# The S5 branch in plain fp32: two pairs of groups in halves of the array, both steps' outputs from the preceding state, D inside an input product

## The chip, the cores and the metric

The kernel runs on one core of one Trainium2 chip. The metric is the device time of one execution in microseconds; the median of 3 runs before the change is 3122.24 us (3120.36 to 3122.88). Beside the runs there is one profiled execution, whose trace spans 3125.4 us from its first to its last instruction. PE is the matmul engine (PEld its weight loads), DVE the vector engine, ACT the scalar engine, POOL the GpSimd, SP the engine that issues most DMAs.

## What is computed

One layer over 1024 tokens of 2048 channels: RMSNorm, an input projection into two branches and gates, an S5 state-space branch, a gated DeltaNet branch, up-projections, a gated merge, an output projection, a residual, and a last RMSNorm. The change is in the S5 branch. It has 64 groups of 16 channels with 64 complex states each, and is linear up to the GELU:

```python
bu_re = jnp.einsum("blgc,gpc->blgp", ug, bb_re)
bu_im = jnp.einsum("blgc,gpc->blgp", ug, bb_im)
...
_, _, s_re, s_im = lax.associative_scan(combine, (a_re, a_im, bu_re, bu_im), axis=1)
y = (jnp.einsum("blgp,gcp->blgc", s_re, _f32(c_re))
     - jnp.einsum("blgp,gcp->blgc", s_im, _f32(c_im)))
y = y.reshape(bsz, l, D_S5) + _f32(d_skip) * u
y = jax.nn.gelu(y)
y = y * jax.nn.sigmoid(y @ _f32(w_glu))
return y * jax.nn.silu(z)
```

## The kernel before

The tokens are taken in two passes of 512. In each pass the big projections are 128x512 products in float32r, a reduced form of fp32 that takes one run through the array: every weight chunk and every activation is split into a hi and a lo part, and each product is three (hi by hi, hi by lo, lo by hi). These "large products" stand on PE in the order of a list of units (q, k, v, z of one head, merge gates, u of one S5 tile, and so on). Weights stream in halves of 512 KB through three buffers `raw`; ACT writes `whi`, DVE writes `wlo`, one chunk for every 12 large products.

Everything else is background work, written as generators: the S5 tiles, the delta rule's preparation and chain, epilogues. After each three large products `pump` lets every lane take one step, if a planner's clock (class `Clock`, a rough model of the engines) says that what the step needs is ready and that DVE isn't too far ahead. So the planner decides where between the large products a step is written; in the program each engine's order is then fixed, and semaphores keep the data right.

S5 works on 8 tiles of 128 channels per pass, each tile 4 pairs of groups. Time is taken in double steps, so a pass has 256 of them:

- `s5_setup` (L593) makes the constants once, in the first pass: the input matrix of each pair (both steps of a double step, hi in `vh_d`, lo in `vl_d`), the output matrices `ft_d` and a product `q0_d` of an output and an input matrix, all kept in DRAM. Its 64 products for `q0_d` are 32 columns wide.
- `s5_epi` (L853) splits u of a tile into hi and lo, even and odd steps, and stores it stacked by pairs (`us_d`) and as it is (`uf_d`).
- `s5_load` (L872) brings `us_d`, `vh_d`, `vl_d` from POOL's queue, `q0_d` and `ft_d` from SP's.
- `s5_gen` (L885), for each pair: an input product of four float32r products (two on 128 rows, two on 64) into bank 6; on DVE a rotation by tables of cos and sin, two scans, the rotation back, into `sx`; then five fp32 products into 32 columns of bank 7. The even step's output comes from the preceding state and the input (`q0`), the odd step's from the state at that step. After four pairs come D times u (two DVE operations on `uf_d`), the GELU, a split into hi and lo, and a store to `yg_d`.

Banks 6 and 7 belong to S5. The delta rule has small fp32 products of its own; the prediction uses two of its loops in `d_prep`. At L1172 four products in one 32x32 strip of the array follow each other, then four in the next. At L1204 two strips take turns, product by product:

```python
for c in range(4):
    PE.matmul(pu[o:o + 32, c, 0:32], lhsT=gs[o + 32:o + 64, c, 0:32], ...)
    PE.matmul(pu[o + 32:o + 64, c, 0:32], lhsT=U[o + 32:o + 64, c, o + 32:o + 64], ...)
```

All instructions are recorded through one helper, so the profile gives L134 for each; groups are told apart by the names of their tiles. `G0a` and `G0b` are the two blocks that hold all S5 tiles, `p` is PSUM, `M` the delta rule's block, `X` and `Y` the activations, `Y` also the scratch of the setup.

Of the kernel before, what the change touches and what calls it, by code (L numbers as in the profile page):

```python
# [36 lines left out]
P = 128  # L37
T = 512          # tokens per pass
NPASS = 2
KT = 16          # k tiles of D_MODEL  # L40
# [53 lines left out]
class Timed:  # L94
# [3 lines left out]
    def __getattr__(self, name):  # L98
# [4 lines left out]
        def g(*a, **k):  # L103
# [6 lines left out]
            if self.key == "PE":  # L110
                if name == "transpose":
                    c = 0.11
                elif k["rhs"].dtype == F32R:
                    c = n / 2400
                else:
                    c = max(n / 600, 0.06) * (0.3 if o.shape[0] <= 32 else 0.5 if o.shape[0] <= 64 else 1.0)
# [30 lines left out]
def kernel(  # L147
# [83 lines left out]
    causal = cpool.tile([P, P], F32, name="causal")      # 1 where partition <= column  # L231
# [20 lines left out]
    vec = cpool.tile([P, 121], F32, name="vec")   # per-channel vectors, one column per tile  # L252
# [16 lines left out]
    vh_d = dram.tile([32, 64, 256], F32, name="vh_d")  # L269
    vl_d = dram.tile([32, 64, 256], F32, name="vl_d")  # L270
    us_d = dram.tile([8, 4, P, 256], F32, name="us_d")   # tile, pair, (hi/lo, even/odd, channel), step
    uf_d = dram.tile([8, P, 1024], F32, name="uf_d")
    ft_d = dram.tile([8, P, 512], F32, name="ft_d")
    q0_d = dram.tile([32, 32, 32], F32, name="q0_d")
    cs_d = dram.tile([32, P, 512], F32, name="cs_d")
    # [4 chunks, 129 rows, 128]: with a row of padding the diagonal blocks lie at one stride
# [4 lines left out]
    ts_d = dram.tile([16, P, T], F32, name="ts_d")  # L281

# [8 lines left out]
    def exp_parts(xin, n, scr):  # L291
        """s, q with exp(x) = s + s*q, on a [128, n] tile; scr: [128, 5n] of scratch."""
# [17 lines left out]
        # two factors, so that the result underflows as exp does  # L310
# [24 lines left out]
    # Half units of [128, 1024]; each gives two chunks of [128, 512], split into hi and lo.  # L335
# [41 lines left out]
    # the first two units share their k loop, and so their chunks alternate  # L377
# [21 lines left out]
    def w_prep():  # L399
# [42 lines left out]
    now = [0.0]            # head being projected, with the share of its units done  # L442
# [34 lines left out]
    def later(o, i):  # L477
        """a store, issued once its data should be there"""
# [114 lines left out]
    def s5_setup(ga, gb, yb):  # L593
        """ga, gb, yb: scratch of [128, 5120], [128, 3072] and [128, 8192]."""
# [66 lines left out]
        # input factor (abar - 1) / lam  # L661
# [14 lines left out]
        # turns per double step, 2 * theta / (2 pi), as fhi + flo  # L676
# [14 lines left out]
        def cmul(dst, c_re, c_im, a_re, a_im):  # L691
            """dst(ri, half) <- c * a; dst returns output views by half of the partitions"""
# [21 lines left out]
        for q4_ in range(8):  # L714
            oo = ((t1f, t2f), (bre_f, bim_f))
            for i in range(2):
# [6 lines left out]
                o, o2 = oo[i][0][0:64, :], oo[i][1][0:64, :]  # L723
                S.activation(o.bitcast(F32R), pb[0:64, :], AF.Copy)
                tt(o2.bitcast(F32R), pb[0:64, :], o, SUB)
            yield
            for i in range(2):
                q2 = 2 * q4_ + i
                for d, o in zip((vh_d, vl_d), oo[i]):
                    SP.dma_start(d[2 * q2:2 * q2 + 2].rearrange("q k m -> k q m"),  # L730
                                 o[0:64, :].rearrange("k (q m) -> k q m", q=2))
# [3 lines left out]
        ft = yb[:, 3072:7168].rearrange("p (i f m) -> p i f m", i=8, f=4)  # L735
# [11 lines left out]
        for i in range(8):  # L747
# [6 lines left out]
        v1 = yb[:, 0:1024].rearrange("p (i q m) -> p i q m", i=8, q=4)  # L754
# [34 lines left out]
    s5w = {}  # L789
# [874 lines left out]
```

## Time and profile before

| what | value |
|---|---|
| median of 3 runs | 3122.24 us |
| span of the profiled execution | 3125.4 us |
| mean granted PE clock | 0.996 |
| input products of S5 (`p<-G0b`, 256 columns) | 256 records, 4 for each pair |
| output products of S5 (`p<-G0a` and `p<-G0b,G0a`, 32 wide, 256 columns) | 640 records, 10 for each pair |
| DMA | 140 GB/s on average |

A product in float32r leaves one record on PE, one in plain fp32 two. The records of PE overlap, since a product is recorded until its last result has gone through the array; what a product costs is read from the distance between starts, not from the length of its record. In the timeline a row merges neighbouring instructions of one kind: its start, the time to the end of the last one, and their number.

### The profile page before, as it was taken

How to read it: one execution, taken by the hardware profiler on the slowest of the kernel's cores; microseconds unless marked ns; L12 is line 12 of the kernel's file. 1: busy time of each engine (PE TensorE's matmuls, PEld its weight loads, DVE VectorE, ACT ScalarE, POOL GpSimd, SP SyncE). 2: the span in 40 equal slices, each digit the busy share in tenths (PEclk: the TensorE clock that was granted, in tenths of full speed). 3: DMA queues.
4: the chain of work that ended last, by engine and by line, in shares of the span. 5: the costliest groups of instructions: out<-in, count | busy, mean ns of one | idle time of the engine just before them, and what ended most of it. 6: DMA issues, size and time to landing. Idle time of an engine off the chain costs nothing.

```text
span 3125.4 us, 43212 instructions
## 1 busy us (share of the span) xinstructions
PE 3091.6 (99%) x16222; PEld 2435.1 (78%) x16222; DVE 1689.8 (54%) x3124; ACT 1140.8 (37%) x2445; POOL 482.7 (15%) x922
## 2 busy tenths in 40 slices
PE   8999999999999999999999999999999999999998
PEld 6887777777777788888877777777777788888887
DVE  5756667766766522553453575566556543226542
ACT  5454444444443222334333334333333322223331
POOL 3432122312200000000042221222122000000000
PEclk9999999999999999999999999999999999999999
DMA  6554545555455644446355455535545564445541
GB/s 163 150 156 119 132 114 127 148 135 144 111 153 162 195 118 124 146 142 219 122 168 136 110 135 133 148 104 136 147 112 141 137 199 132 118 122 152 176 170 56
DMA packets 608980, 438.24 MB, mean 140 GB/s; under 512 B 60489, under 2 KB 535810, under 8 KB 606850
## 3 DMA queue, kind: packets, MB, share of 16 engines
q1 hardware_dynamic: 584962, 406.11, 45.8%
q0 software_dynamic: 23808, 29.37, 4.4%
q8 instruction: 128, 2.10, 0.3%
q14 instruction: 82, 0.67, 0.1%
HBM read 355.05 MB, written 80.35 MB: 139 GB/s over the span
## 4 chain that ended last, share of the span: by engine, by line
PE 91%; DMA 3%; DVE 1%; ACT 1%; POOL 1%; issue 1%; SPq 0%; DVEq 0%; POOLq 0%; ACTq 0%
PE p L134 91%; DMA G0b<-vl_d 2%; POOL M L134 1%; DVE M L134 1%; ACT M L134 0%; SPq L134 0%; POOL G0b L134 0%; DMA vh_d<-G0b 0%; DVE tmp L134 0%; ACT whi L134 0%; DMA raw<-in_w_in_dram 0%; DVE wlo L134 0%; DVE G0a L134 0%; DMA out_dram<-M 0%; ACT G0b L134 0%
## 5 line engine op out<-in xcount | busy, mean ns | idle before, releaser
L134 PE MATMUL p<-X,whi 128*128 128x512 f32 (+1 forms) x4432 | 1401.6, 399 | 1.9 <-DVE whi L134 0.8
L134 DVE TENSOR_TENSOR wlo<-raw,whi 128x512 fp32r<-128x512 f32 x920 | 633.0, 701 | 688.9 <-ACT whi L134 686.8
L134 PEld LDWEIGHTS p<-X,whi 128*128 128x128 f32 (+1 forms) x4432 | 801.5, 188 | 179.7 <-issue 19.2
L134 PE MATMUL p<-X,wlo 128*128 128x512 f32 (+1 forms) x2184 | 853.3, 391 | 0.3 <-DVE wlo L134 0.2
L134 ACT ACTIVATE whi<-raw 128x512 fp32r<-128x512 f32 x917 | 558.0, 625 | 593.2 <-PE p L134 561.3
L134 PE MATMUL p<-Y,whi 128*128 128x512 f32 (+1 forms) x1808 | 571.7, 398 | 0.9 <-ACT p L134 0.9
L134 PEld LDWEIGHTS p<-X,wlo 128*128 128x128 f32 x2184 | 411.4, 188 | 89.6 <-DVE wlo L134 0.9
L134 PEld LDWEIGHTS p<-Y,whi 128*128 128x128 f32 (+1 forms) x1808 | 328.0, 187 | 74.7 <-issue 7.4
L134 PE MATMUL p<-Y,wlo 128*128 128x512 f32 x896 | 350.2, 391 | 0.0
L134 ACT ACTIVATE tmp<-p 128x512 f32<-128x512 f32 x160 | 95.6, 597 | 480.4 <-PE p L134 469.9
L134 POOL TENSOR_SCALAR smalls<-smalls 128x4 f32<-128x4 f32 (+1 forms) x58 | 16.8, 289 | 1377.3 <-DVE smalls L134 1104.2
L134 POOL TENSOR_TENSOR M<-M 32x28 f32<-32x28 f32 (+8 forms) x492 | 182.2, 370 | 268.6 <-DMA M<-lu_d 215.8
L134 DVE TENSOR_TENSOR G0a<-G0a 128x256 f32<-128x256 f32 (+1 forms) x432 | 211.0, 525 | 3.8
L134 PEld LDWEIGHTS p<-M 32*32 32x32 f32 (+2 forms) x3072 | 153.1, 123 | 66.8 <-ACT M L134 27.9
L134 PEld LDWEIGHTS p<-Y,wlo 128*128 128x128 f32 x896 | 168.3, 188 | 36.8 <-DVE wlo L134 0.3
L134 PE MATMUL p<-M 32*32 32x32 f32 (+3 forms) x3072 | 186.9, 215 | 2.5 <-DMA M<-tu_d 1.0
L134 ACT ACTIVATE M<-p 32x128 f32<-32x128 f32 (+3 forms) x337 | 99.2, 298 | 181.7 <-PE p L134 175.6
L134 DVE TENSOR_TENSOR G0a<-p,G0a 128x512 f32<-128x512 f32 x128 | 82.3, 685 | 129.1 <-PE p L134 129.0
L134 PE MATMUL p<-G0a 128*32 128x256 f32 x512 | 133.1, 382 | 0.0
L134 DVE SCALAR_TENSOR_TENSOR tmp<-tmp,vec 128x512 f32<-128x512 f32 x144 | 112.1, 778 | 20.5 <-ACT tmp L134 17.1
L134 PEld LDWEIGHTS p<-G0a 128*32 128x32 f32 x512 | 50.9, 109 | 62.4 <-issue 7.6
L134 DVE TENSOR_TENSOR_SCAN G0a<-rho,scar,G0a 128x256 f32<-128x256 f32 x128 | 90.2, 746 | 0.0
(212 smaller groups left out, 2879.1 us busy)
## 6 DMA issues: line engine op xcount, KB each, us to landing
raw<-in_w_in_dram SPq DMA_DIRECT2D x324, 512.0 KB, 4.0
raw<-in_w_out_dram SPq DMA_DIRECT2D x56, 512.0 KB, 3.9
raw<-in_dn_w_up_dram SPq DMA_DIRECT2D x32, 512.0 KB, 4.2
raw<-in_s_w_up_dram SPq DMA_DIRECT2D x32, 512.0 KB, 3.9
td_d<-tmp SPq DMA_DIRECT2D x32, 256.0 KB, 2.0
M<-tu_d SPq DMA_DIRECT2D x32, 256.0 KB, 3.9
cs_d<-G0a SPq DMA_DIRECT2D x32, 256.0 KB, 3.1
G0b<-us_d POOLq DMA_DIRECT2D x16, 512.0 KB, 7.5
```

The source lines that it names most:

```text
L134: return f(*a, **k)
```

## The change

- The input product of a pair is plain fp32 on the 64 rows of its inputs (2 steps x 2 groups x 16 channels); `vh_d`, `vl_d` and the hi and lo of u are gone. Two pairs are taken together: one in rows 0 to 63, the other in rows 64 to 127, into banks 6 and 7.
- Both steps' outputs come from the state before the double step, so the output matrices are C times A and C times A squared, 64 columns for a pair (2 steps x 32 channels). The two pairs' products go to columns 0 to 63 and 64 to 127.
- What the two steps' inputs add to both outputs, D included, is one product on the whole array with a 128x128 matrix for two pairs (`w0_d`), which the setup makes with 128 products 32 or 64 columns wide.
- u is stored once, in fp32, with even and odd steps apart (`uf_d` is gone). The tile's loads are on SP's queue, with two buffers for u, `ft` and `w0`; the next tile's are issued behind the second two pairs' input product if its u is there by then.
- y stays with even and odd steps apart up to the last merge; the epilogues of z, of the S5 gate and of the last sum read or write every second element instead.
- The planner's clock prices an fp32 product on up to 64 rows at half.

The core of the diff:

```diff
@@ s5_setup
-            S.activation(ft[:, i, 2, :], pb[:, 0:P], AF.Copy)
-            S.activation(ft[:, i, 3, :], pb[:, P:2 * P], AF.Copy, scale=-1.0)
...
+        G.memset(gb[:, 0:2048], 0.0)
+        yield
+        for hf in range(2):
+            pb = bank((6, 7)[hf])
+            pw = pb.rearrange("p (j e c) -> p j e c", j=8, e=2)
+            for j in range(8):
+                for a in range(2):
+                    pr = 2 * (hf * 8 + j) + a
+                    for e in range(2):
+                        for ri in range(2):
+                            m = nb[:, pr, ri].rearrange("p e g c -> p (e g c)")
+                            PE.matmul(pw[64 * a:64 * a + 32 + 32 * e, j, e, :], lhsT=m[:, 0 if e else 32:64],
+                                      rhs=ft[:, pr, ri, 1, :], start=(ri == 0), stop=(ri == 1))
+                if j % 2 == 1:
+                    yield
...
+        for j in range(16):
+            wj = w0[:, j].rearrange("p a e c -> p (a e c)")
+            stt(wj, ident, dd[:, j:j + 1], wj, MUL, ADD)
@@ s5_load
-        G.dma_start(us, us_d[t].rearrange("q p n -> p q n"))
-        for hh in range(2):
-            G.dma_start(vh[64 * hh:64 * hh + 64], vh_d[4 * t:4 * t + 4].rearrange("q k m -> k q m"))
-            SP.dma_start(q0[64 * hh:64 * hh + 32], q0_d[4 * t:4 * t + 4].rearrange("q k m -> k q m"))
-        G.dma_start(vl, vl_d[4 * t:4 * t + 4].rearrange("(a b) k m -> (b k) a m", b=2))
-        SP.dma_start(ft, ft_d[t].rearrange("p (f m) -> p f m", f=4))
+        i = t % 2
+        SP.dma_start(s5w["us"][i], us_d[t].rearrange("p (s n) -> p s n", s=2))
+        SP.dma_start(s5w["v"], v_d[t].rearrange("p (s m) -> p s m", s=2))
+        SP.dma_start(s5w["ft"][i].rearrange("p q r m -> p (q r m)"), ft_d[t])
+        SP.dma_start(s5w["w0"][i].rearrange("p s m -> p (s m)"), w0_d[t])
@@ s5_gen
-        for q in range(4):
...
-            pV = bank(6)
             for ri in range(2):
-                o = pV[:, ri * 256:(ri + 1) * 256]
-                PE.matmul(o, lhsT=vh[:, q, ri * P:(ri + 1) * P], rhs=us[:, q, :],
-                          start=True, stop=False)
-                PE.matmul(o, lhsT=vl[lr, q // 2, ri * P:(ri + 1) * P],
-                          rhs=us[lr, q, :],
-                          start=False, stop=True)
+                for h in range(2):
+                    r = slice(64 * h, 64 * h + 64)
+                    PE.matmul(pV[h][:, ri * 256:(ri + 1) * 256], lhsT=vv[r, sl, ri * P:(ri + 1) * P],
+                              rhs=us[r, sl, :], start=True, stop=True)
+            if sl == 1 and t < 7 and ("u", t + 1) in done:
+                yield
+                yield from s5_load(t + 1)
...
-            for e in range(2):
-                o = pY[32 * q:32 * q + 32, e * 256:(e + 1) * 256]
-                for ri in range(2):
-                    PE.matmul(o, lhsT=ft[:, 2 * e + ri, 32 * q:32 * q + 32], rhs=sx[:, ri, e:e + 256],
-                              start=(ri == 0), stop=(e == 1 and ri == 1))
-                if e == 0:
-                    PE.matmul(o, lhsT=q0[:, q, :], rhs=us[:, q, :].bitcast(F32), start=False, stop=True)
+            pY = bank(6)
+            PE.matmul(pY[:, 0:256], lhsT=w0[:, sl, :], rhs=us[:, sl, :], start=True, stop=False)
+            for ri in range(2):
+                for h in range(2):
+                    PE.matmul(pY[64 * h:64 * h + 64, 0:256], lhsT=ft[:, 2 * sl + h, ri, :],
+                              rhs=s5w["sx"][h][:, ri, 0:256], start=False, stop=(ri == 1))
+            yield
+            S.activation(us[:, sl, :], pY[:, 0:256], AF.Copy)
...
-        stt(Gf, Af, vec[:, DSK + t:DSK + t + 1], pY, MUL, ADD)
-        stt(Af, Bf, vec[:, DSK + t:DSK + t + 1], Gf, MUL, ADD)
```

How the program's order moves, first on PE in the first pass, where one pair's outputs and the next pair's input product stand among the large products. Before (columns x length of each product; `p6` and `p7` are the S5 banks):

```order
L134 MATMUL p7_539_4642<-G0a_257_2174 32x256 x2
L134 MATMUL p7_539_4642<-G0b_258_2175,G0a_257_2174 32x256
L134 MATMUL p7_539_4642<-G0a_257_2174 32x256 x2
L134 MATMUL p0_544_4683<-X0_6_173,whi_537_4631 128x512 x2
L134 MATMUL p0_544_4683<-X0_6_173,wlo_538_4632 128x512
L134 MATMUL p6_550_4752<-G0b_258_2175 128x256 x4
```

After, on the same engine in the same pass, two pairs' outputs and, some large products later, the next two pairs' input product:

```order
L135 MATMUL p6_560_4831<-G0b_258_2231,G0a_257_2230 128x256
L135 MATMUL p6_560_4831<-G0a_257_2230,G0b_258_2231 64x256 x4
L135 MATMUL p1_557_4810<-X0_6_171,whi_550_4726 128x512 x2
...
L135 MATMUL p1_557_4810<-X0_6_171,wlo_553_4753 128x512
L135 MATMUL p6_565_4877<-G0b_258_2231 128x256
L135 MATMUL p7_566_4878<-G0b_258_2231 128x256
L135 MATMUL p6_565_4877<-G0b_258_2231 128x256
```

Nine products for one pair have become nine for two, the two halves take turns, and the outputs share bank 6 with the input product.

Second, the setup's products on PE. Before they stand in one lump; its two middle rows are all 64:

```order
L134 MATMUL p4_242_2012<-ident_75,M0_64_533 128x128 x4
L134 MATMUL p6_243_2017<-Y0_2_148,G0a_8_175 32x32 x32
L134 MATMUL p7_244_2052<-Y0_2_148,G0a_8_175 32x32 x32
L134 MATMUL p0_228_1920<-X1_7_174,whi_229_1921 128x512 x2
L134 MATMUL p0_228_1920<-X1_7_174,wlo_230_1922 128x512
```

After, the end of one of eight lumps:

```order
L135 MATMUL p6_209_1748<-Y0_2_146,G0a_8_173 32x32 x2
L135 MATMUL p6_209_1748<-Y0_2_146,G0a_8_173 64x32 x2
L135 MATMUL p6_209_1748<-Y0_2_146,G0a_8_173 32x32 x2
L135 MATMUL p6_209_1748<-Y0_2_146,G0a_8_173 64x32 x2
L135 MATMUL p0_184_1586<-X1_7_172,whi_185_1587 128x512 x2
```

Their width changes every two products now, and their number is doubled.

Third, a tile's loads. Before, on POOL's queue, between two of the delta rule's operations there, and no weight loads:

```order
L134 COPY M0_64_533<-M0_64_533 32x256
L134 DMA G0b_258_2175<-us_d_121 128x4x256
L134 DMA G0b_258_2175<-vh_d_119 64x4x256 x2
L134 DMA G0b_258_2175<-vl_d_120 128x2x256
L134 TENSOR_TENSOR dhl_171<-gth_166,causal_82 128x256
```

After, on SP's queue, between two weight loads (`raw`):

```order
L135 DMA raw_737_6331<-in_w_in_dram 128x8x128
L135 DMA G0b_258_2231<-us_d_120 128x512
L135 DMA G0b_258_2231<-v_d_119 128x512
L135 DMA G0b_258_2231<-ft_d_121 128x512
L135 DMA G0a_257_2230<-w0_d_122 128x256
L135 DMA raw_744_6393<-in_w_in_dram 128x8x128
```

The four transfers of a tile stand in the one queue that also feeds the weights.

More of the change, by code (lines that the diff above doesn't have):

```diff
@@ L268 @@
     yg_d = dram.tile([8, P, 2, T], F32, name="yg_d")
[L269 to L272, printed above, removed]
+    v_d = dram.tile([8, P, 512], F32, name="v_d")
+    us_d = dram.tile([8, P, 512], F32, name="us_d")
     ft_d = dram.tile([8, P, 512], F32, name="ft_d")
-    q0_d = dram.tile([32, 32, 32], F32, name="q0_d")
+    w0_d = dram.tile([8, P, 256], F32, name="w0_d")
     cs_d = dram.tile([32, P, 512], F32, name="cs_d")
@@ L281, with part @@
     ts_d = dram.tile([16, P, T], F32, name="ts_d")
+    def part(d, off, *dims):
+        a = d[:, :, :] if len(d.shape) == 3 else d[:, :, :, :]
+        return bass.AP(tensor=a.tensor, offset=a.offset + off, ap=[list(x) for x in dims])
     def diag_blocks(d):
@@ L789 @@
+        SP.dma_start(ft_d.rearrange("i p m -> p i m"), yb[:, 3072:7168].rearrange("p (i m) -> p i m", i=8))
+        yield
     s5w = {}
     def s5_views():
-        ga, gb = block("G0a", [P, 5120], F32), block("G0b", [P, 3072], F32R)
+        ga, gb = block("G0a", [P, 5120], F32), block("G0b", [P, 3072], F32)
         o = [0]
@@ L885, in s5_gen @@
     def s5_gen(t, ps_):
[L886 removed]
+        us, ft, w0 = (s5w[k][t % 2] for k in ("us", "ft", "w0"))
+        vv = s5w["v"]
         A, B, Gt = s5w["A"], s5w["B"], s5w["G"]
@@ new lines, in s5_gen @@
+            if sl == 1 and t < 7 and ("u", t + 1) in done:
+                yield
+                yield from s5_load(t + 1)
+            yield
+            for h, pair in enumerate(pairs):
+                cs = s5w["cs"][pair % 2]
+                sx = s5w["sx"][h]
+                if ps_ == 0:
+                    yield from hold(lambda: s5n["tab"] > pair)
+                pv3 = pV[h].rearrange("p (a n) -> p a n", a=2)
+                cb = cs[:, 0:1, :].broadcast_to([P, 2, 256])
+                sb = cs[:, 1:2, :].broadcast_to([P, 2, 256])
+                tt(A, pv3, cb, MUL)
+                tt(B, pv3, sb, MUL)
+                yield -1
+                tt(Gt[:, 0, :], A[:, 0, :], B[:, 1, :], ADD)
+                tt(Gt[:, 1, :], A[:, 1, :], B[:, 0, :], SUB)
+                yield -1
+                for ri in range(2):
+                    V.tensor_tensor_scan(A[:, ri, :], rho[:, pair:pair + 1].broadcast_to([P, 256]),
+                                         Gt[:, ri, :], scar[:, pair, ri:ri + 1], op0=MUL, op1=ADD)
+                yield -1
+                tt(Gt, A, cb, MUL)
+                tt(B, A, sb, MUL)
+                yield -1
+                tt(sx[:, 0, 1:257], Gt[:, 0, :], B[:, 1, :], SUB)
+                tt(sx[:, 1, 1:257], Gt[:, 1, :], B[:, 0, :], ADD)
+                V.tensor_copy(sx[:, :, 0:1], scar[:, pair, :].unsqueeze(2))
+                V.tensor_copy(scar[:, pair, :].unsqueeze(2), sx[:, :, 256:257])
+                if ps_ > 0 and pair + 2 < 32:
+                    later(cs.rearrange("p a n -> p (a n)"), cs_d[pair + 2])
+                s5n["pair"] = pair + 1
+                yield -1 if h == 0 else 0
@@ L969, in s5_gen @@
         yield
-        SP.dma_start(yg_d[t, :, 0, :], Af)
-        SP.dma_start(yg_d[t, :, 1, :], Bf)
+        for a in range(2):
+            for e in range(2):
+                SP.dma_start(part(yg_d, t * 131072 + a * 32768 + e * 256, (1024, 32), (512, 2), (65536, 2), (1, 256)),
+                             AB[64 * a + 32 * e:64 * a + 32 * e + 32, :]
+                             .rearrange("p (h s n) -> p h s n", h=2, s=2))
         yield
@@ L1541 @@
             elif kind in ("z", "zs"):
-                add("epi", 0, silu_epi(pb, (zd_d if kind == "z" else zs_d)[i]), 0.0)
+                add("epi", 0, silu_epi(pb, (zd_d if kind == "z" else zs_d)[i], kind == "zs"), 0.0)
                 if kind == "z":
```

175 lines of the change are left out of this document (69 added, 106 removed).

## The prediction

> **What bounds the kernel now.** I read the page from the top: busy time by engine, then the chain of work that ended last, then who PE waited for.
>
> ```profile
> span 3125.4 us, 43212 instructions
> PE 3091.6 (99%) x16222; PEld 2435.1 (78%) x16222; DVE 1689.8 (54%) x3124; ACT 1140.8 (37%) x2445; POOL 482.7 (15%) x922
> PE 91%; DMA 3%; DVE 1%; ACT 1%; POOL 1%; issue 1%; SPq 0%; DVEq 0%; POOLq 0%; ACTq 0%
> ```
>
> PE is busy from end to end and carries 91% of the chain. A busy PE need not be a fast one, so the second question is whether it ever stands still. The longest rows of the view of waits for PE:
>
> ```profile
> PE p L134 <- DVE M L134: 6.5, 6, 3.7
> PE p L134 <- POOL tmp L134: 5.3, 1, 5.3
> PE p L134 <- DMA G0b<-vh_d: 4.5, 3, 3.0
> PE p L134 <- DMA G0b<-vl_d: 2.2, 4, 0.7
> ```
>
> With the shorter rows it is under 25 us of 3125. So the time is the sum of what PE's instructions take, and a change in PE's own work goes through to the end one for one, as long as nothing new makes PE wait. Everything below is therefore a price per piece of S5 work on PE, read as the delay that it puts between the large products around it.
>
> **The input product before.** One pair of groups, on the timeline of PE (start, length to the end of the last, count):
>
> ```profile
> 903.16 0.39 PE L134 MATMUL p<-X,wlo 128*128 128x512 f32 x1
> 903.39 0.62 PE L134 MATMUL p<-X,whi 128*128 128x512 f32 x2
> 903.84 0.39 PE L134 MATMUL p<-X,wlo 128*128 128x512 f32 x1
> 904.07 1.21 PE L134 MATMUL p<-G0b 128*128 128x256 f32 x4
> 905.21 0.73 PE L134 MATMUL p<-X,whi 128*128 128x512 f32 x2
> 905.78 0.39 PE L134 MATMUL p<-X,wlo 128*128 128x512 f32 x1
> ```
>
> Three large products take 903.84 - 903.16 = 0.68 us when nothing lies between. With four S5 products between they take 905.78 - 903.84 = 1.94 us, so a pair costs 1.26 us.
>
> **The outputs before.** The same reading for a pair's five output products, which are plain fp32 and leave two records each:
>
> ```profile
> 875.79 0.40 PE L134 MATMUL p<-X,wlo 128*128 128x512 f32 x1
> 876.12 1.05 PE L134 MATMUL p<-G0a 128*32 128x256 f32 x4
> 877.01 0.59 PE L134 MATMUL p<-G0b,G0a 128*32 128x256 f32 x2
> 877.44 1.03 PE L134 MATMUL p<-G0a 128*32 128x256 f32 x4
> 878.39 0.73 PE L134 MATMUL p<-X,whi 128*128 128x512 f32 x2
> 878.96 0.40 PE L134 MATMUL p<-X,wlo 128*128 128x512 f32 x1
> ```
>
> 878.96 - 875.79 - 0.68 = 2.49 us. Two records take 877.44 - 877.01 = 0.43, so a record of 256 columns takes **0.215 us**, although only 32 of the array's 128 columns give a result. Ten of them are 2.15; the other **0.34 us** is paid for going into a part of the array and back (the first starts 0.33 after its forerunner instead of 0.227, and the two large products behind take 0.57 instead of 0.45).
>
> Two pairs cost 2 x (1.26 + 2.49) = 7.50 us. There are 64 pairs over both passes: 32 x 7.50 = **240 us** of S5 on PE.
>
> **The same two pairs after.** Input product: four fp32 products on 64 rows, eight records. Outputs: one on the whole array (two records) and four on 64 columns (eight records). All are 256 columns long, so each record is 0.215 by the row above. All hangs on whether the records of the two halves run beside each other. No row of before shows two halves in turn, but there are 32x32 strips, at two places in the delta rule that issue equal products:
>
> ```profile
> 317.35 0.39 PE L134 MATMUL p<-X,wlo 128*128 128x512 f32 x1
> 317.67 0.89 PE L134 MATMUL p<-M 32*32 32x32 f32 x32
> 318.49 0.73 PE L134 MATMUL p<-X,whi 128*128 128x512 f32 x2
> ...
> 325.96 0.39 PE L134 MATMUL p<-X,wlo 128*128 128x512 f32 x1
> 326.27 0.60 PE L134 MATMUL p<-M 32*32 32x32 f32 x32
> 326.81 0.73 PE L134 MATMUL p<-X,whi 128*128 128x512 f32 x2
> ...
> L134 PE MATMUL p<-Y,G0a x128: 196/196/218, 202.6 to 206.6; 128*32 128x32 f32 x128
> ```
>
> The last row is 128 records in one strip: 4.0 / 127 = 0.0315 us each, so 32 in a row would need 31 x 0.0315 + 0.19 = 1.17 us. The first run (L1172, four products in one strip, then four in the next) takes 0.89; the second (L1204, two strips in turn) takes 0.60. From first start to last start that is 0.41 us for 32 records, 0.013 each: under half of 0.0315. Strips that alternate product by product, the order in which the changed code issues its halves, do run beside each other, fp32 pairs of records included. I take this for both kinds of halves.
>
> The Trainium skill speaks against a part of it: "TensorE: Matmul & The Clock Gate", Part 3, says that matmuls keep strict program order and never pass one another, only weight loads do. Under that rule the second record of a product waits for its first, and the other half's product starts only with it, so eight records fill five record times instead of four. For L1204 that would be 16 x 0.0315 = 0.50 us from start to start; the rows give 0.41, so the trace leans against it.
>
> Going in and out: the loads of 128 and of 32 columns last
>
> ```profile
> L134 PEld LDWEIGHTS p<-X,wlo 128*128 128x128 f32 x2184 | 411.4, 188 | 89.6 <-DVE wlo L134 0.9
> L134 PEld LDWEIGHTS p<-G0a 128*32 128x32 f32 x512 | 50.9, 109 | 62.4 <-issue 7.6
> ```
>
> so a switch with a 128-column load laid bare is 0.34 + 0.08 = 0.42, and with 64 columns some 0.37.
>
> - Input product: 4 x 0.215 + 0.42 = 1.28 us with halves side by side, 8 x 0.215 + 0.42 = 2.14 one after another.
> - Outputs: 2 x 0.215 + 4 x 0.215 + 0.37 = 1.66, or 2.52.
>
> Together 2.94 us, or 4.66. Times 32: 94 or 149. The saving is **146 us** if halves overlap, **91 us** if they do not.
>
> **What the change adds.** (a) The setup's products: 64 before (the 128 records, 4.0 us), 128 after, and widths of 32 and 64 columns take turns every two products, 64 changes in all. Low bound: 256 x 0.0315 = 8.1, or +4. High bound: each change pays half of the 0.34 (64 x 0.17 = 10.9), 64-column loads add about 0.03 to 128 records (3.8), and the run is cut into eight lumps (7 x 0.34 = 2.4): +21. The nearest row is the switch in the output run, so I take **+17**. "TensorEngine Tiling (Array Packing)" of the Trainium skill, Key Properties, says that changing the tiling mode drains the engine while changing the tile does not; by it I would have the upper figure, and no row shows a change from 32 to 64 columns.
>
> (b) Loads of a tile. The 6.7 us of waits on vh_d and vl_d go. One of them also slowed what followed:
>
> ```profile
> 1691.01 2.21 PE L134 MATMUL p<-G0b 128*128 128x256 f32 x4 [3.04 <-DMA G0b<-vh_d]
> 1694.17 0.63 PE L134 MATMUL p<-X,wlo 128*128 128x512 f32 x1
> 1695.45 0.63 PE L134 MATMUL p<-X,wlo 128*128 128x512 f32 x1
> SPq L134 <- DVE wlo L134: 1088.0, 344, 14.6
> raw<-in_w_in_dram SPq DMA_DIRECT2D x324, 512.0 KB, 4.0
> G0b<-vh_d POOLq DMA_DIRECT2D x32, 256.0 KB, 8.4
> ```
>
> After 3.04 us idle three large products took 1.28 us instead of 0.68. The changed loads leave POOL's queue for SP's, where they stand behind weight loads that wait for DVE (3.2 us on average, 14.6 at most); behind them stand the next weight loads, which have three buffers of cover. A DMA lands faster from SP (4.0 against 8.4). Bounds: nothing, and 1 us at each of 16 tiles. I take 4, so the net is **-3 us**.
>
> (c) DVE's share. Its work per pair is not cut, but it now has to be done twice between an input product and its outputs:
>
> ```profile
> L134 DVE TENSOR_TENSOR G0a<-p,G0a 128x512 f32<-128x512 f32 x128 | 82.3, 685 | 129.1 <-PE p L134 129.0
> L134 DVE TENSOR_TENSOR G0a<-G0a 128x256 f32<-128x256 f32 x288 | 114.3, 434 | 2.8
> L134 DVE TENSOR_TENSOR_SCAN G0a<-rho,scar,G0a 128x256 f32<-128x256 f32 x128 | 90.2, 746 | 0.0
> L134 DVE TENSOR_TENSOR G0a<-G0a 128x512 f32<-128x512 f32 x144 | 96.7, 708 | 1.1
> L134 DVE TENSOR_TENSOR wlo<-raw,whi 128x512 fp32r<-128x512 f32 x920 | 633.0, 701 | 688.9 <-ACT whi L134 686.8
> PEld p L134 <- DVE G0a L134: 4.3, 12, 0.4
> ```
>
> Per pair 2 x 0.685 + 4 x 0.434 + 2 x 0.746 + 2 x 0.708 and two small copies (some 0.35) = 6.4 us, two pairs 12.7. Weights take 0.70 in every 12 large products (4 x 0.68 = 2.72 us), 26% of DVE, so two pairs need 12.7 / 0.74 = 17.2 us, more where the convolution stands between. In the second pass the program has 72 to 105 large products there, 16.3 to 24 us. Before, a pair had 30 to 90 (6.8 to 20 us) for 6.4 / 0.74 = 8.6, and yet the outputs' weight loads waited for DVE only 4.3 us in all, by the last row; but a double run of DVE work lets a delay grow twice as long, and the time that slow S5 products gave DVE goes as well. Bounds 0 and 25 us (1.6 at each of the 16 places of the second pass); I take **+10 us**. Dropping the two D operations and the lo half of u helps DVE but not the end.
>
> **Sum.** -146 + 17 - 3 + 10 = -122 us. On the execution with its span of 3125.4 us that gives a span of 3003; no other time of that execution is shown, and the runs' median, 3122.2, lies 3.2 below its span. So **3000 us** is forecast.
>
> **Rivals.**
> - *Halves one after another.* The array may share something between halves of 64 rows, both of which write all 128 outputs, that strips do not; no row shows it. -91 instead of -146: 3055. If only one kind overlaps, 27 us are lost: 3027. For: halves are not in the trace. Against: the strips of L1204 overlap.
> - *Strict order.* Five record times for four, 0.215 twice in 32 places: +14, so 3014.
> - *Tile loads late, slower than before.* Each of the 16 tiles begins with loads queued on SP behind a weight load. If PE stands for T us at each, the gain is 122 - 16 x T: gone from T = 7.6 us on. For: the 14.6 us row, and an idle PE then runs at half speed, as behind the 3.04 us above. At T = 10 the time is 3160. Against: the worst wait of the old loads was 3.0 us, and SP's average wait is 3.2.
>
> **How the numbers follow.** Forecast 0.68, both kinds in series 0.09, one kind in series 0.10, strict order 0.08, something slower 0.03, gain eaten to nothing 0.02. The forecast's own bounds: with (a) at +4, (b) at -7, (c) at 0 it is 2973; with +21, +9, +25 it is 3031. That span also holds strict order and one kind in series. A little more room above, for one of these together with a high (a) or (c), gives 2973 to 3040, which leaves out series of both kinds, the slower case and the tails, under two in ten. A measurement of this kernel tells about 0.2% (6 us) from no change: faster 0.95, within 0.02, slower 0.03.
>
> **What would show it.** Right: an input run of 8 records with some 1.3 us between the large products around it, outputs with 1.7; PE's waits still near 25 us. Wrong: 2.1 and 2.5 (halves in series), PE rows waiting on DMA into G0b (loads), weight loads of outputs waiting on DVE G0a or scar beyond 25 us (DVE), a setup that takes PE over 30 us or under 10.

## The result, and the profile after

The changed kernel takes 3030.18 us (median of 4 runs, 3029.73 to 3030.53), the kernel before beside it 3122.56 (3120.36 to 3125.38): a ratio of 0.970, 95% interval 0.9687 to 0.9715. That is 92 us less. The forecast was 122 less, 3000 us, in a range of 2973 to 3040. The span of the profiled execution is 3027.8 us, 97.6 less than before. It lies 2.4 below the median, that of before lay 3 above its own; so of the 30 us by which the forecast missed, 25 are in the spans (3003 forecast, 3027.8 measured), and the rest is this offset.

The page of the changed kernel: span, busy time by engine, the chain that ended last:

```profile
span 3027.8 us, 42544 instructions
PE 2974.2 (98%) x16030; PEld 2391.6 (79%) x16030; DVE 1662.4 (55%) x3082; ACT 1152.2 (38%) x2483; POOL 449.3 (15%) x857
PE 85%; DVE 7%; POOL 2%; ACT 2%; issue 1%; DMA 1%; SPq 0%; DVEq 0%; POOLq 0%; ACTq 0%
```

PE is still busy 98% of the span, but its part of the chain fell from 91 to 85% and DVE's rose from 1 to 7%. So the page already says that something waits for DVE now. Who, is in the view of waits (us in total, times, longest):

```profile
PE p L135 <- ACT M L135: 13.6, 14, 1.7
PE p L135 <- DVE M L135: 8.9, 8, 3.9
PE p L135 <- DVE wlo L135: 7.9, 2, 7.7
PE p L135 <- DVE G0a L135: 0.7, 2, 0.3
PE p L135 <- DMA G0b<-v_d: 0.3, 1, 0.3
...
PEld p L135 <- ACT M L135: 45.6, 101, 2.1
PEld p L135 <- DVE G0a L135: 1.8, 3, 0.8
```

The loads of a tile cost 0.3 us in place of 6.7, and the S5 outputs hardly wait for DVE (`G0a`). The rows on `ACT M` have grown; before, they were

```profile
PE p L134 <- ACT M L134: 0.7, 2, 0.5
PEld p L134 <- ACT M L134: 28.3, 89, 0.9
```

New is one wait of 7.7 us on `wlo`. All of PE's rows add to 44.1 us, 24.3 before. "PE's waits still near 25 us" was one of the forecast's signs of being right, and this one failed.

**S5 on PE.** Outputs of two pairs, then an input product of two pairs, on PE's timeline:

```profile
619.07 0.39 PE L135 MATMUL p<-X,wlo 128*128 128x512 f32 x1
619.30 0.59 PE L135 MATMUL p<-G0b,G0a 128*128 128x256 f32 x2
619.82 1.09 PE L135 MATMUL p<-G0a,G0b 128*64 128x256 f32 x8
620.84 0.73 PE L135 MATMUL p<-X,whi 128*128 128x512 f32 x2
621.40 0.39 PE L135 MATMUL p<-X,wlo 128*128 128x512 f32 x1
...
624.60 0.39 PE L135 MATMUL p<-X,wlo 128*128 128x512 f32 x1
624.91 1.13 PE L135 MATMUL p<-G0b 64*128 64x256 f32 x8
625.98 0.73 PE L135 MATMUL p<-X,whi 128*128 128x512 f32 x2
626.55 0.39 PE L135 MATMUL p<-X,wlo 128*128 128x512 f32 x1
```

Read as before: 621.40 - 619.07 - 0.68 = 1.65 us for the outputs, 626.55 - 624.60 - 0.68 = 1.27 us for the input product. Forecast were 1.66 and 1.28. Eight records of 0.215 would be 1.72 us alone; the halves do run beside each other.

**The setup.** One of its eight lumps of 32 records takes 2.43 us:

```profile
202.11 2.43 PE L135 MATMUL p<-Y,G0a 128*32 128x32 f32 x32
204.47 0.73 PE L135 MATMUL p<-X,whi 128*128 128x512 f32 x2
```

**The end of the setup.** Where S5's setup must be finished, what is left of it is written out at once ("drained"), here twelve operations (products and sums) of 1024 columns on DVE. DVE's timeline, then PE's:

```profile
211.00 14.71 DVE L135 TENSOR_TENSOR Y<-Y 128x1024 f32<-128x1024 f32 x12
...
226.29 2.49 DVE L135 TENSOR_TENSOR wlo<-raw,whi 128x512 fp32r<-128x512 f32 x4
...
227.03 0.80 PE L135 MATMUL p<-X,wlo 128*128 128x512 f32 x1 [7.70 <-DVE wlo L135]
```

The weights' lo parts stand behind 14.71 us of setup, and PE waits 7.70 us for the first of them.

**The delta rule.** One of the places behind the row on `ACT M`, in the second pass, again DVE, ACT and PE:

```profile
1980.78 1.39 DVE L135 TENSOR_TENSOR_SCAN G0a<-rho,scar,G0a 128x256 f32<-128x256 f32 x2
1982.20 1.29 DVE L135 TENSOR_TENSOR G0a<-G0a 128x512 f32<-128x512 f32 x2
1983.41 0.68 DVE L135 TENSOR_TENSOR wlo<-raw,whi 128x512 fp32r<-128x512 f32 x1
1984.02 0.69 DVE L135 SCALAR_TENSOR_TENSOR M<-tmp 128x512 f32<-128x512 f32 x1
...
1984.73 0.63 ACT L135 ACTIVATE M<-M 128x512 f32<-128x512 f32 x1 [3.29 <-DVE M L135]
...
1983.30 0.39 PE L135 MATMUL p<-X,wlo 128*128 128x512 f32 x1
1985.42 1.05 PE L135 MATMUL p<-ones,M 128*128 128x1 f32 x8 [1.73 <-ACT M L135]
```

DVE is busy without a gap with S5's scans and rotations; the last operation of the convolution, `M<-tmp`, stands behind them, ACT squares its result, and PE, which is to sum the squares, stands still for 1.73 us. The wait is entered under ACT, but ACT itself had waited 3.29 us for DVE. So a row of the waits names the last hand, not the cause.

**PE's clock.** The trace also holds the clock that PE was granted. Behind this wait it is half for 3.41 us (stretch and its length; busy time and number of instructions of PE, its weight loads, DVE, ACT and POOL; PE's clock; DMA), and two large products last 1.22 us there in place of 0.62:

```profile
1987.94:1991.35 3.41, 3.41 (x10) 1.98 (x11) 0.88 (x3) 0.90 (x2) 1.62 (x5) 0.50 0.04 9
1989.82 1.22 PE L135 MATMUL p<-X,whi 128*128 128x512 f32 x2
```

In the second pass each of the six waits for `ACT M` over 1 us (1.17 to 1.73) has such a stretch of 3.4 or 6.8 us behind it, at most 2.6 us later. A wait of 1.47 us on another row, at 1821 us, has none, so the trace gives no length from which on a wait brings one. From the first large product to the last PE is at half clock for 30.7 us, before the change for 10.2. What that costs can be estimated as half of the part of these stretches in which PE was busy: 13.3 us, 4.8 before.

**Where the time went, summed over PE.** From the starts of all of PE's records: a run of other instructions between two large products costs the time from the start of the large product before it to the start of the second one behind it, less 2 x 0.227 us. Summed by what a run holds, in us:

| kernel | runs with S5 products | with setup products | with other small products | large product to large product |
|---|---|---|---|---|
| before | 261.3 | 13.8 | 302.1 | 10.4 |
| after | 117.0 | 32.4 | 320.3 | 20.4 |
| difference | -144.3 | +18.6 | +18.2 | +10.0 |

The differences add to -97.5, the difference of the spans. (Some runs hold S5 and delta-rule products, 22 before and 11 after, so the first and the third column aren't quite apart. The second column also has the setup's transposes: the runs with products for `q0_d` or `w0_d` alone are 4.8 us before and 25.4 after. The third has what lies before the first large product, 34.3 and 33.3 us.)

By cause, the difference comes out nearly the same: S5's products on PE -146.6 us (32 x (7.50 - 1.27 - 1.65)), the setup +18.6, PE's waits +19.8 (24.3 to 44.1), its half clock +8.5 (4.8 to 13.3, the estimate above); together -99.7, 2 us from the measured.

### The profile page after: what moved, and what is told of

It reads as the page before. It is cut to its first block, busy times and chain, and to the rows that moved or that the text cites. A ratio compares the mean times of both kernels' runs of the same rounds, so it can differ in the third digit from the quotient of the medians.

```text
span 3027.8 us, 42544 instructions
## 1 busy us (share of the span) xinstructions
PE 2974.2 (98%) x16030; PEld 2391.6 (79%) x16030; DVE 1662.4 (55%) x3082; ACT 1152.2 (38%) x2483; POOL 449.3 (15%) x857
## 4 chain that ended last, share of the span: by engine, by line
PE 85%; DVE 7%; POOL 2%; ACT 2%; issue 1%; DMA 1%; SPq 0%; DVEq 0%; POOLq 0%; ACTq 0%
PE p L135 85%; DVE G0a L135 2%; POOL M L135 2%; DVE M L135 2%; DVE wlo L135 1%; DVE tmp L135 1%; ACT M L135 1%; DMA raw<-in_w_in_dram 0%; DVE Y L135 0%; POOL smalls L135 0%; DMA M<-tu_d 0%; SPq L135 0%; ACT whi L135 0%; ACT L135 0%; ACT tmp L135 0%
## 5 line engine op out<-in xcount | busy, mean ns | idle before, releaser
L135 PEld LDWEIGHTS p<-X,wlo 128*128 128x128 f32 x2184 | 411.7, 189 | 97.6 <-DVE wlo L135 9.1
L135 POOL TENSOR_TENSOR M<-M 32x28 f32<-32x28 f32 (+8 forms) x492 | 190.7, 388 | 289.4 <-DMA M<-lu_d 194.2
L135 DVE TENSOR_TENSOR G0a<-p,G0a 128x512 f32<-128x512 f32 x128 | 82.0, 682 | 13.4 <-PE p L135 10.8
L135 PE MATMUL p<-whi,G0a 128*128 128x512 f32 x280 | 88.5, 391 | 0.0
L135 PE MATMUL p<-whi,X 128*128 128x512 f32 x256 | 82.2, 393 | 0.0
```

The source lines that it names most:

```text
L135: return f(*a, **k)
```

## Experiments

The expectations name kernels by their batch: "the fourth kernel" is number 5 here, "the former kernel" in 7 and "the first kernel of this batch" in 8 and 9 are number 6. All times are medians; the kernel before ran beside each batch (3123 to 3127 us), so kernels of different batches are compared by their ratios too. The changed kernel's is 0.9701.

**1. Order of the halves.** Both loops over `ri` and `h` are exchanged, so that both products of one half come first, then both of the other.

```diff
-            for ri in range(2):
-                for h in range(2):
+            for h in range(2):
+                for ri in range(2):
```

> In both S5 products the two halves no longer alternate: upper half re, upper half im, then lower half re, lower half im. Nothing is left out. Theory (the halves run side by side whatever their order, because products of different halves do not wait for each other): an input product stays near 1.16 us and an output slot near 1.54 us, the time stays within 3 us of 3030. Rival (products run strictly in order and only a neighbour of the other half is overlapped): of 4 input records of 0.215 us per half pair the middle ones overlap only, so each product costs one to four more records, 0.2 to 0.86 us in each of 64 places, and the kernel takes 3044 to 3085 us.

Measured: 3029.23 us, ratio 0.9699 (0.9685 to 0.9712), the same as the changed kernel. Its input product on the timeline:

```profile
627.03 0.39 PE L135 MATMUL p<-X,wlo 128*128 128x512 f32 x1
627.35 1.14 PE L135 MATMUL p<-G0b 64*128 64x256 f32 x8
628.42 0.73 PE L135 MATMUL p<-X,whi 128*128 128x512 f32 x2
628.99 0.39 PE L135 MATMUL p<-X,wlo 128*128 128x512 f32 x1
```

628.99 - 627.03 - 0.68 = 1.28. The first product of the lower half stands behind two products of the upper in the program, and still the eight records fill four record times. The outputs take 1.66 us (median; 1.65 in the changed kernel), so the same holds for halves of the columns. The rival with a strict order is out.

**2. No halves.** Both groups' pairs take rows 0 to 63, and both outputs go to columns 0 to 63. The one product with `w0` is split into two halves of columns, which isn't shown here:

```diff
-lhsT=vv[r, sl, ri * P:(ri + 1) * P], rhs=us[r, sl, :]
+lhsT=vv[0:64, sl, ri * P:(ri + 1) * P], rhs=us[0:64, sl, :]
...
-PE.matmul(pY[64 * h:64 * h + 64, 0:256], lhsT=ft[:, 2 * sl + h, ri, :], ...
+PE.matmul(pY[0:64, 0:256], lhsT=ft[:, 2 * sl + h, ri, :], ...
```

> The changed kernel with both groups' pairs in the same half of the array, so that nothing can run side by side: the input products of both take rows 0 to 63, and the output products of both go to columns 0 to 63 (the output of w0 is split into two halves of columns). This leaves out half of the input and puts both outputs into one half: only the time is meant. Theory (the change's saving rests on the halves running side by side): an input product takes 8 records of 0.215 us, 2.1 us with its switch in place of 1.27, an output slot 2.5 in place of 1.65, 1.7 us x 32 = 55 us more, 3085 us; a little less, 3065 to 3085, if the longer products give DVE time and the waits for ACT M fall. Rival (the saving came from the switches and fewer instructions and not from halves side by side): within 15 us of 3030.

Measured: 3076.86 us, ratio 0.9846 (0.983 to 0.9862), 47 us more than the changed kernel. Its input product on the timeline:

```profile
636.67 0.39 PE L135 MATMUL p<-X,wlo 128*128 128x512 f32 x1
636.99 1.99 PE L135 MATMUL p<-G0b 64*128 64x256 f32 x8
638.91 0.74 PE L135 MATMUL p<-X,whi 128*128 128x512 f32 x2
639.49 0.40 PE L135 MATMUL p<-X,wlo 128*128 128x512 f32 x1
```

and its waits:

```profile
PE p L135 <- ACT M L135: 13.6, 14, 1.8
...
PEld p L135 <- ACT M L135: 45.6, 101, 2.2
```

639.49 - 636.67 - 0.68 = 2.14, the figure that the forecast had for halves in series; the outputs' median is 2.505 (forecast 2.52). In the sum over PE the runs with S5 rise by 52.5 us. So side by side is worth about 50 us of this kernel. And a second thing follows: S5 now takes PE 50 us longer, but the waits for `ACT M` are what they were. PE's speed in S5 has no part in them, so they aren't why the 47 us stay under the theory's 55.

**3. The widths in the setup.** Within a lump all 32-column products come first, then all 64-column ones:

```diff
-            for j in range(8):
-                for a in range(2):
-                    pr = 2 * (hf * 8 + j) + a
-                    for e in range(2):
+            for j0 in range(0, 8, 2):
+                for e in range(2):
+                    for j in (j0, j0 + 1):
+                        for a in range(2):
+                            pr = 2 * (hf * 8 + j) + a
```

> The 128 small setup products of w0 are issued grouped by the width of their output (32 or 64 columns) inside each of the eight lumps: 2 changes of width in a lump in place of 8. Same products, nothing left out. Theory (the lumps take 2.44 us where 16 products of 0.06 to 0.07 us would take about 1.1, because each change of the array's tiling empties it, some 0.15 us a change): a lump falls to 1.4 to 1.8 us, the eight together save 5 to 8 us, 3022 to 3025 us. Rival (each product costs 0.15 us whatever its neighbour): lumps stay at 2.4 us and the time within 1 us of 3030.

Measured: 3019.52 us, ratio 0.9671 (0.9657 to 0.9684), 10.7 us less than the changed kernel. A lump now:

```profile
193.10 1.07 PE L135 MATMUL p<-Y,G0a 128*32 128x32 f32 x32
194.11 0.73 PE L135 MATMUL p<-X,whi 128*128 128x512 f32 x2
```

A lump falls from 2.43 to 1.07 us, and the gain is larger than the theory had it. The starts of the single records, which the merged rows don't show, say why: two things came together.

- *Fewer changes.* In the changed kernel's lump eight records, four of each width, repeat every 0.590 us. Within one width records follow each other every 0.0315 us (32 columns) or 0.058 (64). Four of each are 0.358, which leaves 0.232 for two changes: 0.116 us a change, less than the 0.15 expected. Six changes fewer are 0.70 of the 1.36 us.
- *Columns side by side.* Products of one width for different columns of the array now stand next to each other, and their records start in twos, 13 ns apart at first: the 16 records of 32 columns take 0.395 us to the first one of 64 columns, where one after another they would need 16 x 0.0315 = 0.50 and a change. The expectation didn't name this. It is the other 0.66 us.

The eight lumps give 32.4 - 21.6 = 10.8 us, all of the gain, about half of it by each. With another order of the loops the setup's products cost 21.6 - 13.8 = 7.8 us more than before the change, in place of 18.6.

**4. The block at the end of the setup.** Of the twelve operations that multiply the output matrices by the step, the first six (now in a helper `ft_step`) go ahead of the `w0` products, the last six to POOL.

```diff
+        yield from ft_step(1, 0)
...
-        for e, d in ((1, 0), (0, 1)):
-            re, im = ft[:, :, 0, e, :], ft[:, :, 1, e, :]
-            tt(v1, re, bc(ar, 32), MUL)
...
+        yield from ft_step(0, 1, eng=G)
```

> The twelve 128x1024 multiplications of the output matrices by the step leave DVE's block at the end of the setup: the first six stand before the w0 products, the last six on POOL. Same arithmetic. Theory (PE's wait of 7.7 us for wlo at 219 us comes from DVE's block of 14.7 us that the setup's drain lets out at once): the wait falls under 1 us and the time by 6 to 8 us, to 3022 to 3024 us. Rival (the wait only moves: POOL's six take some 2 us each and the first S5 tile, or the products behind the drain, wait for them): the time stays within 2 us of 3030.

Measured: 3023.67 us, ratio 0.9682 (0.9668 to 0.9695), 6.5 us less. The row of the waits:

```profile
PE p L135 <- DVE wlo L135: 1.2, 2, 1.0
```

7.9 became 1.2. The cause of that wait was the block.

**5. Honest prices.** Only the planner's prices of DVE and ACT change, to what the trace of the changed kernel shows; the largest error was the scan, planned at 0.40 us and taking 0.74.

```diff
-_VG = {"V": (0.07, 1.04e-3), "G": (0.14, 2.1e-3), "S": (0.05, 0.9e-3)}
-_VF = {"V": (0.1, 0.6e-3), "G": (0.12, 1.1e-3), "S": (0.05, 0.9e-3)}
+_VG = {"V": (0.17, 1.04e-3), "G": (0.14, 2.1e-3), "S": (0.19, 0.83e-3)}
+_VF = {"V": (0.14, 0.7e-3), "G": (0.12, 1.1e-3), "S": (0.19, 0.83e-3)}
...
-"tensor_tensor_scan": {"V": (0.07, 1.28e-3)},
+"tensor_tensor_scan": {"V": (0.2, 2.13e-3)},
```

> Only the planner's prices change: DVE and ACT operations and the scan at what the trace of the changed kernel shows (scan 0.75 us for 256 in place of 0.40, 128x512 tensor_tensor 0.70 in place of 0.60, ACT 128x512 0.61 in place of 0.51). Theory (DVE is behind its plan, so that the delta rule's products wait for ACT M and DVE M, 22.5 us of waits against 7.2 before, and PE's weight loads wait 45.6 us for ACT M): these waits fall by 10 to 20 us and the time with them, to 3010 to 3020 us. Rival (the waits come from the length of the chains and not from the plan): the time stays within 3 us of 3030 or rises, since the planner puts S5 further back.

Measured: 3042.79 us, ratio 0.9742 (0.9729 to 0.9755), 12.6 us more: a miss. Its waits say part of why, and half of the theory holds:

```profile
PE p L135 <- DMA G0a<-yg_d: 15.2, 1, 15.2
PE p L135 <- ACT M L135: 0.5, 1, 0.5
...
PEld p L135 <- ACT M L135: 1.1, 2, 0.7
```

The waits for `ACT M` are gone (13.6 to 0.5, 45.6 to 1.1). In their place PE stands once for 15.2 us at the S5 gate of the first pass, which needs all of S5's `yg`. In the written order S5's first input product of that pass now stands behind 950 large products in place of 674, and its last output behind 4202 of 4204, in place of 3221: a planner that believes in a slower DVE lets the setup in later, and all of S5 with it.

The wait for `yg` isn't the whole loss. PE is at half clock for 78.5 us (30.7 in the changed kernel), 27.3 of them around this wait and 27.3 from 214.8 us on, where PE is busy throughout:

```profile
214.80:242.00 27.20, 27.20 (x222) 23.27 (x222) 3.26 (x13) 3.62 (x10) 0.74 (x2) 0.50 0.01 1
```

By the same estimate as above the half clock costs 26.3 us in place of 13.3. What lowered it at 214.8 us stays open: PE's waits in the 4 us before are 0.3 us and less.

**6. Both edits of the setup together**, experiments 3 and 4.

> The two edits that helped, together: w0 products grouped by width, and the multiplications by the step taken out of DVE's block (six ahead of the w0 products, six on POOL). Nothing left out. They saved 10.7 and 6.5 us alone. Theory (they are different places, a run of small products and a wait behind it): the savings add, 3012 to 3014 us. Rival (shorter lumps leave less time for DVE's work behind the same main products, so that part of the wait returns): 3016 to 3019 us.

Measured: 3011.72 us, ratio 0.9632 (0.9619 to 0.9646). The savings add, although a part of the wait for `wlo` is back (3.0 us, 1.2 in experiment 4). Experiments 7 to 11 start from this kernel.

**7. Honest prices in the second pass alone**, where the setup has no part.

```diff
+PRICES = [prices(_VG["V"], _VF["V"], _VG["S"], (0.07, 1.28e-3)),
+          prices((0.17, 1.04e-3), (0.14, 0.7e-3), (0.19, 0.83e-3), (0.2, 2.13e-3))]
...
     for ps_ in range(NPASS):
+        COST.update(PRICES[ps_])
```

> The former kernel, with the planner's prices of DVE and ACT as measured, from the second pass on only. Theory (the delta rule's products of the second pass wait for ACT M because DVE is behind its plan; in the fourth kernel these waits of 1.2 to 1.7 us were gone, and its loss of 12.6 us came from a single place, the end of the first pass, where S5 had been put too late and its last outputs, then yg, were waited for 22 us): the waits for ACT M of the second pass go, 5 to 12 us less than the former kernel, 3001 to 3008 us. Rival (S5 comes late at the end of the second pass too, and its drain takes the gain back): the former kernel's time or up to 15 us more.

Measured: 2985.15 us, ratio 0.9548 (0.9535 to 0.9561), 26.6 us less than number 6, more than twice what was expected:

```profile
PE p L135 <- ACT M L135: 2.2, 5, 0.4
...
PEld p L135 <- ACT M L135: 16.6, 43, 0.9
```

Over PE the runs with S5 fall from 115.7 to 97.4 and the other small ones from 322.5 to 311.5, while the large ones rise by 3.4. PE's waits for `ACT M` account for 10.5 us of the gain (12.7 to 2.2). Its half clock accounts for some 6.8 more (at half for 6.8 us in place of 20.5, which the estimate prices at 3.4 and 10.2). Some 9 us are left that no row of PE's waits names; the weight loads' row on `ACT M` fell by 28.3 (44.9 to 16.6), but how much of that delayed PE isn't shown.

**8. A looser rule for S5 in place of it**: honest prices in both passes, and S5 let in while DVE stands up to 3 us behind.

```diff
-"s5": 1.0, "tab": 1.0
+"s5": 3.0, "tab": 1.0
```

> As the first kernel of this batch, with the measured prices in both passes and S5 let in while DVE stands up to 3 us behind PE in place of 1. Theory (the loss of the fourth kernel came from the rule that lets S5 in only while DVE is within 1 us, which honest prices make rarer): the wait for yg at the end of the first pass goes, the waits for ACT M stay small, 3000 to 3008 us. Rival (what S5 takes on DVE is then late for the delta rule again): 3012 to 3016 us, with waits for ACT M and DVE M as in the changed kernel.

Measured: 3030.36 us, ratio 0.9688 (0.9675 to 0.9701): a miss. S5's last outputs of the first pass still stood behind 4202 large products, and PE waited 14.8 us for `yg`. The rule for S5 wasn't what held it.

**9. Less work on DVE.** The two additions ahead of each scan go to POOL, old prices.

```diff
-                tt(Gt[:, 0, :], A[:, 0, :], B[:, 1, :], ADD)
-                tt(Gt[:, 1, :], A[:, 1, :], B[:, 0, :], SUB)
+                tt(Gt[:, 0, :], A[:, 0, :], B[:, 1, :], ADD, eng=G)
+                tt(Gt[:, 1, :], A[:, 1, :], B[:, 0, :], SUB, eng=G)
```

> As the first kernel of this batch, with the two 128x256 additions ahead of each scan on POOL in place of DVE, in all 64 groups' pairs: 2 x 0.43 us less on DVE each, 55 us in all. Theory (it is DVE's load that makes the delta rule's products wait): the waits for ACT M and DVE M fall by 5 to 15 us and the time with them, to 2998 to 3008 us. Rival (POOL takes longer for them, and the longer chain of S5 is waited for, at the outputs or the end of a pass): 3012 to 3025 us.

Measured: 3000.53 us, ratio 0.9596 (0.9583 to 0.9609), 11.2 us less than number 6:

```profile
PE p L135 <- ACT M L135: 5.4, 9, 1.1
...
PEld p L135 <- ACT M L135: 30.4, 80, 1.6
```

12.7 and 44.9 in number 6 became 5.4 and 30.4. A lighter DVE takes a part of these waits away, with ACT's work as it was: that speaks for DVE as their cause, though their rows name ACT. It isn't DVE's load alone, since the planner sees the lighter DVE too and writes another order. And PE is at half clock for only 3.4 us in place of 20.5; by the estimate that is 8.5 of the 11.2 us (10.2 to 1.7).

**10. Numbers 7 and 9 together.**

> Everything that helped in one kernel: w0 products grouped by width, the step's multiplications out of DVE's block, measured prices in the second pass, and the two additions ahead of each scan on POOL. Nothing left out. The last two took 26.6 and 11.2 us from 3011.7 us alone. Theory (both act on the same waits for DVE and ACT, so they overlap in part): 2972 to 2982 us. Rival (with honest prices DVE's load no longer matters, and POOL's longer time is then waited for): 2985 us or more.

Measured: 2984.56 us, ratio 0.9551 (0.9537 to 0.9566), no better than number 7. The time is the rival's: with honest prices in the second pass a lighter DVE brings nothing more. That POOL's longer time is waited for in its place isn't shown; the weight loads' row on POOL's `G0a` is 1.1 us.

**11. The setup let in earlier, honest prices in both passes.** `SETUP` is how far DVE may be behind PE when a step of the setup is written.

```diff
-SETUP = 2.0
+SETUP = 10.0
```

> As the kernel with both edits of the setup, with the measured prices in both passes, and the setup's work let in while DVE stands up to 10 us behind PE in place of 2. In the written order S5's first input product then stands behind 695 large products and its last output of the first pass behind 4070; with the measured prices alone these were 950 and 4202 (the end), with the old prices 683 and 3221. Theory (the measured prices lost in the first pass only because they held the setup back, so that S5 came to its end too late): no wait for yg, and the gain of the second pass kept, 2975 to 2990 us. Rival (the setup's work, let in early, is in the way of the weights and the delta rule of the first pass, or S5 placed late has its own price): 2995 us or more.

> The same with 6 us in place of 10: first input product behind 695 large products, last output of the first pass behind 4118. By the theory within 5 us of the run with 10 us, 2975 to 2990 us; by the rival, if it is the setup's work that is in the way, less than the run with 10 us by 5 us or more.

Measured: 2993.51 us with 10 (0.9578, 0.9565 to 0.9591) and 2988.76 with 6 (0.9564, 0.9551 to 0.9577). No wait for `yg` over 2 us is left in either, so it was the late setup that put S5 at the end of the first pass. The waits with 6:

```profile
PE p L135 <- DMA G0b<-yg_d: 2.0, 3, 0.8
PE p L135 <- DMA G0a<-yg_d: 1.4, 3, 0.7
...
PEld p L135 <- ACT M L135: 0.8, 2, 0.4
```

With 10 the time lies between the theory's range and the rival's, with 6 in the theory's. The waits for `ACT M` are almost gone, and yet neither is faster than number 7, which keeps 16.6 us of them for its weight loads; all of PE's waits together are 29.6 us with 6 and 29.9 in number 7. With 6, the runs with other small products fall by another 4.5 us against number 7 (307.0), but those with S5 rise by 4.7 (102.1) and the time between large products by 2.4 (21.4). What honest prices win in the first pass is lost there again. PE's clock is enough to account for it: at half for 30.7 us with 10, 20.5 with 6 and 6.8 in number 7, by the estimate 13.9, 9.8 and 3.4 us, while the two are 8.4 and 3.6 us behind number 7. The intervals of 6 and 10 overlap. Fastest of all are numbers 7 and 10, some 45 us below the changed kernel.

## Why the prediction was right, and where its sum was not

- **S5 on PE, -146 us: right, and for its reason.** A pair of pairs costs 1.27 + 1.65 us (forecast 1.28 + 1.66), 32 x (7.50 - 2.92) = 146.6. Experiment 2 took the halves away and got the forecast's own 2.14 and 2.52. The inference from 32x32 strips to halves of 64 rows or columns held. (The 0.013 us a record of L1204 are not of two strips alone: there a second pair of strips starts before the first is done. Within a pair two records start 7 ns apart, every 0.032 us, and on that the inference rests.)
- **Strict order, a rival of 0.08: out.** Experiment 1 leaves it nowhere to stand. The forecast's own row of L1172 spoke against it more clearly than that of L1204: four strips with eight records each would need 28 x 0.0315 = 0.88 us from first to last start in strict order, and the row gives 0.89 - 0.19 = 0.70. The rivals with halves in series fall by the timeline and by experiment 2.
- **(a) Setup, +17: right in size, its parts less so.** +18.6 measured. A change of width costs 0.116 us by the starts in the lumps, where 0.17 was taken, and inside the eight lumps there are 56 of them, 6.5 us. The 128 records of 64 columns take 0.058 us in place of 0.0315, 3.4 us (3.8 in the forecast). The sign "a setup that takes PE over 30 us" didn't come: the column's 32.4 us hold transposes, the products alone are 25.4.
- **(b) Loads, -3: a little too careful.** The row on `v_d` is 0.3 us in place of 6.7, so the 4 us set against it didn't come. The slower case, S5's tiles waited for behind SP's queue, shows nowhere.
- **(c) DVE's share, +10: the mis-sized term.** Forecast as a delay of S5's own outputs, it wasn't there (weight loads waited 1.8 us for `G0a`, 4.3 before). DVE's work came late for others: for the delta rule's products, +18.2 us in the runs with other small products, and for the large products, +10.0, of which 7.7 is the one wait at the end of the setup. These 28.2 us have no term of their own. By cause, PE's waits rose by 19.8 us where (b) and (c) together had +7, and its half clock cost 8.5 us more, which the sum put at nothing, although the forecast had read the half speed off the place behind the 3.04 us. The runs with S5 came out 5.3 better than the sum had them with (b) and (c) (-144.3 against -139) and the setup 1.6 worse; 28.2 - 5.3 + 1.6 = 24.5, which is the difference between -122 and -97.5. That the time still lies in the range owes something to luck: the range had room above for a large (c) and for halves in series, and a cause that it doesn't name has filled it.
- **The step that failed** is the question asked for (c): who waits for S5's DVE work? The forecast looked at the product that reads its result. DVE took its work in the order written at both places quoted above, so whoever stands behind it waits as well: `M<-tmp`, `wlo`. And a wait was priced by its idle time alone, without the slower PE behind it. Of the two reasons given there, "the time that slow S5 products gave DVE goes as well" fell with experiment 2: giving PE's 50 us back left the rows on `ACT M` as they were. That DVE's plan counts is shown by 7; 9 speaks for its load. That it is the double run of DVE work in particular, the other reason given, fits the place quoted above but wasn't tried by itself.

## What to carry to other kernels

When a change shortens an engine's work, price what stays on the other engines by who stands *behind* it in their queues, not only by who reads it, and follow a wait's row one hand further back than the engine it names. Where a planner sets the order, a change of the work is a change of its inputs as well: compare its prices with the trace after each such change, and see where a more honest price moves work to before trusting it (12.6 us lost or 26.6 won here, by where it was applied). Price a wait of PE with the stretch at half clock behind it. Small products of two widths go in groups by width, and those for different columns next to each other.

## What was unexpected of the hardware

- Products of different halves of the array don't only alternate, they pass one another: with the order of experiment 1 the records start in twos, 13 ns apart, each two 216 to 320 ns behind the last two, while the program had both products of one half first. (The trace doesn't say which half a record belongs to; that eight of them fill four record times does.) "TensorE: Matmul & The Clock Gate" of the Trainium skill, Part 3, says that matmuls start and end in program order, with no reordering. By that rule the lower half's first record would wait for the start of the upper half's fourth, and the eight would fill seven record times, 1.5 us; the measured four speak against it for halves of the rows, and outputs of 1.66 us for halves of the columns.
- A change between 32 and 64 columns costs 0.116 us, nearly four of the records of 0.0315 us around it. "TensorEngine Tiling (Array Packing)" of the Trainium skill, Key Properties, says that a change of the tiling mode drains the engine, without a figure; the lumps of the changed kernel agree in that a change costs time, and they give one.
- A short wait of PE cost about twice its idle time here, by the estimate above: behind each of the six waits of 1.17 to 1.73 us for `ACT M` in the second pass the granted clock was 0.5 for 3.4 or 6.8 us.
